# Gate sigmoids and scaled keys computed where their tiles leave PSUM, with the conv norm, the scan's steps and the final scaling dealt out differently

## The chip, the cores and the metric

The kernel runs on one core of a Trainium2 chip. The metric is device time in microseconds (us) for one execution. In what follows PE is TensorE (matrix products into PSUM banks), DVE is VectorE, ACT is ScalarE, POOL is GpSimd, and SP is the engine whose queue issues most of the transfers between SBUF and DRAM.

## The reference

The program is one layer of an encoder on x of 1024 positions and 1024 channels, float32. A projection h W_in feeds a convolution module and a two-direction gated scan; their merge goes back through W_out, and a gated feed-forward part follows.

```python
h = rmsnorm(x); proj = h @ w_in               # columns: glu, q, v, z_f, z_b, og, g_a, g_b
a = glu(glu_in)                               # 512 channels
a = depthwise_conv31(a); a = silu(layernorm(a)); a = a @ pw_w
for z, lb in ((z_f, lb[0]), (z_b, lb[1])):    # 8 heads of 128 channels, each direction
    f   = lb + (1 - lb) * sigmoid(z)          # forget gate, clipped to [1e-6, 1]
    key = (1 - lb) * sigmoid(-z)
    o  += scan(silu(q) * 128**-0.5, key, v, log(clip(f)))
o = rmsnorm(o) * norm_w * silu(og) @ o_w
x = x + (sigmoid(g_a) * a + sigmoid(g_b) * o) @ w_out
x = x + ffn(rmsnorm(x)); out = rmsnorm(x)
```

## The kernel before

All activations lie transposed: channels on the 128 partitions, positions along the free axis in two halves of 512. A number of full precision is kept as two parts (a rounded high part, and the rest), and a product of two such numbers takes three matmuls (`mm3`, L149 to L151). `split` (L125) makes the parts: a CAST on ACT for the high part, a TENSOR_TENSOR on DVE for the low part.

The projection's 128-column tiles are listed in `todo`, in the order in which they are computed: q and og of the eight heads, then v, z_f and z_b head by head, then the merge gates. The first 38 tiles are computed two at a time as 19 "pairs" (`in_pair`, `pair_job`). A pair multiplies a 2 by 2 block of tiles with seven block products instead of eight, each product 12 matmuls of 128x512. The products run in the order 1, 2, 6, 7, 5, 4, 3 and use three PSUM banks: mm, tr, mm, sc, mm, sc, mm. Products that add on to a bank wait until ACT has copied its value before (`A.copy` into `su`, L440). DVE or ACT then finishes the four result tiles (`evac`), and SP stores them to DRAM. Every tile of z is stored raw into `d_z`.

The order on the engines is that in which the program emits its instructions, apart from some that a scheduler may move (`pin` fixes one in its place). Two kinds of work are woven by hand: a `Stream` such as `s_pairs` holds the pieces of the dense products, and `fill(n)` emits n pieces of it between pieces of other work. A piece of a pair is two groups of three matmuls. `later(n, f)` (the list `chores`) calls f after n further pieces. Beside the pairs run the depthwise convolution on DVE (31 taps on 1024 positions, four chunks of channels), and then, for each half, the conv's layer norm. The norm loads four chunks (`cx`) from `d_cv` with SP (L1061), sums them on DVE (L1051, L1053), multiplies by a matrix of ones on PE for the mean (L1065), subtracts, squares on ACT (L1071), forms the reciprocal deviation, multiplies and shifts on DVE, applies silu on ACT (L1079), splits into two parts (`ch`) and stores these to `d_ca` (L1082). The `cx` pages are two buffers of two chunks, so that the loads of the second half follow the last read of the first.

The scan (`scan_inputs`, `Base`, `scan_levels`, `scan_states`, 16 rounds of head and half) follows, woven with the dense tiles that are left (`dense.fill`). `scan_inputs` loads q and the two z tiles; ACT makes sigmoid(-z) (L1163), sigmoid(z) (L1164) and the affine gate (L1165), DVE the clamp and the scaling of the key. `Base` prepares levels of doubling block sizes 1 to 16; `scan_levels` goes on with 32 and 64, with small matmuls on PE (`blocks`, L1281), each after a DVE step `double` that scales keys and queries. At the program's end the down projection's last tiles are transposed back (`turn_out`, L1890), squared and summed on ACT (L1892), and scaled by the final norm's factor (`scale_out`: 640 columns on DVE, L1928, and 384 on ACT, L1926), once all eight column tiles of a part are there.

Of the kernel before, what the change touches and what calls it, by code (L numbers as in the profile page):

```python
# [24 lines left out]
LN_LAST = 12  # L25
# [5 lines left out]
BASE_STEPS = 1  # L31
# [17 lines left out]
def tile_hybrid_encoder(  # L49
# [107 lines left out]
    chores = []  # L157
# [5 lines left out]
    def advance_chores(n=1):  # L163
        for c in list(chores):
            c[0] -= n
            if c[0] <= 0:
                chores.remove(c)
                c[1]()

# [395 lines left out]
    d_z = scratch("d_z", 2, NH, 2)  # L565
# [230 lines left out]
    def store(dst, func=None):  # L796
# [12 lines left out]

    todo = [  # L810
# [7 lines left out]
    todo += [  # L818
        t
        for h in range(NH)  # L820
        for t in (
            (OFF_V + h * DK, store(d_v[h])),
            (OFF_ZF + h * DK, store(d_z[0][h])),
            (OFF_ZB + h * DK, store(d_z[1][h])),
        )
    ]
    todo += [(OFF_GA + i * P, store(d_ga[i], AF.Sigmoid)) for i in range(ND)]
# [162 lines left out]

    def lb_of(d, h):
        return lbw[:, 2, d * NH + h : d * NH + h + 1]
# [63 lines left out]
    for half in range(2):  # L1056
# [18 lines left out]
        rs = next(rstd)  # L1075
        for j, xn in enumerate(xs):
            V.tensor_tensor(xn, xn, rs, op=ALU.mult)
            V.tensor_scalar(xn, xn, vec("lnw", j), vec("lnb", j), op0=ALU.mult, op1=ALU.add)
            A.activation(xn, xn, AF.Silu)  # L1079
            both = gp0.tile([P, 2, H], F32R, tag="gl", name=nm("ch"), bufs=NCW)  # L1080
            for dst, part in zip(d_ca[j][half], split(both[:, 0, :], both[:, 1, :], xn, V)):
                nc.sync.dma_start(dst, part.bitcast(F32))  # L1082
        s_pairs.fill(LN_LAST)
# [62 lines left out]
    kscale = cp.tile([P, 2 * NH], F32, name="kscale")  # L1146
    V.tensor_scalar(kscale, lbw[:, 3, :], DK**-0.5, None, op0=ALU.mult)

# [3 lines left out]
    def scan_inputs(i):  # L1152
# [7 lines left out]
        for d in range(2):  # L1160
            z = page(hp, "zi", 3)
            nc.sync.dma_start(z, d_z[d][h][half])
            A.activation(kG[:, d, :], z, AF.Sigmoid, scale=-1.0)  # L1163
            A.activation(z, z, AF.Sigmoid)  # L1164
            A.activation(f[:, d, :], z, AF.Identity, scale=oml_of(d, h), bias=lb_of(d, h))  # L1165
        V.tensor_scalar(f, f, MIN_FORGET, 1.0, op0=ALU.max, op1=ALU.min)
        return q, f, kG, kscale[:, h : h + NH + 1 : NH]
# [49 lines left out]
    def scan_base(ins):  # L1217


        q, f, kG, ks = ins  # L1220
        qF = hp.tile([P, 2, H], F32, tag="qF", name=nm("qF"), bufs=4)
        D_t = hp.tile([P, 4, 32], F32, tag="D", name=nm("D"), bufs=3)
        for d in range(2):
            V.tensor_scalar(kG[:, d, :], kG[:, d, :], ks[:, d : d + 1], None, op0=ALU.mult)
# [45 lines left out]
    def scan_levels(base, S_t, Tt):  # L1270
# [25 lines left out]
        level(slot(b, 1), A16, row(Q16))  # L1296
# [743 lines left out]
```

## Time and profile before

| | us |
|---|---|
| median of 3 runs (lowest, highest) | 1740.16 (1738.36, 1743.63) |
| the profiled execution, its own time | 1736.41 |
| its span, first to last instruction | 1734.3 |
| PE busy | 1709.2 |
| DVE busy | 1255.9 |
| ACT busy | 830.3 |
| POOL busy | 170.4 |

The granted PE clock was 0.998 of full speed. Rows of the profile name the line, the engine, the operation and the tiles (out<-in, buffer numbers left out). A row of a timeline begins with its start and its length in us, and has in brackets how long the engine had been idle and who ended that. A matmul of 128x512 is listed with some 0.39 us because matmuls are pipelined; how often one starts is what counts. The pairs take the stretch from some 118 to 490 us, the scan that from 490 to 880.

### The profile page before, as it was taken

The numbers are of one execution on the slowest core, as the hardware profiler recorded it, in microseconds if no ns is written. First come the engines' busy times: TensorE is split into PE (matmuls) and PEld (weight loads), VectorE is DVE, ScalarE is ACT, GpSimd is POOL, SyncE is SP. The second block draws the span as 40 slices with busy tenths as digits, with TensorE's granted clock in tenths as the row PEclk, the third lists the DMA queues.
The fourth block names the chain that finished last, engine by engine and source line by source line (L and its number), as shares of the span: only waits on it lengthen the run. The fifth ranks groups of instructions, "written<-read, shape, count | busy, mean of one in ns | idle before, by whom it ended". The sixth has DMA issues, their size and how long they took to land.

```text
span 1734.3 us, 30669 instructions
## 1 busy us (share of the span) xinstructions
PE 1709.2 (99%) x11902; PEld 1415.0 (82%) x11902; DVE 1255.9 (72%) x1937; ACT 830.3 (48%) x1544; POOL 170.4 (10%) x185
## 2 busy tenths in 40 slices
PE   8999999999999999999999999999999999999997
PEld 6878888888788888888878888888888888888787
DVE  5599999746778888888557466667767776657865
ACT  7444443334566777776442245444434433542334
POOL 2211111100000000000000002011111111000110
PEclk9999999999999999999999999999999999999999
DMA  8768888854673444435579466568777776783842
GB/s 288 239 167 184 193 194 193 197 167 154 207 230 104 131 126 132 127 115 192 175 248 333 147 207 205 146 148 170 158 170 160 180 172 153 229 267 107 205 91 98
DMA packets 343751, 308.27 MB, mean 178 GB/s; under 512 B 25262, under 2 KB 255798, under 8 KB 343606
## 3 DMA queue, kind: packets, MB, share of 16 engines
q1 hardware_dynamic: 289590, 267.51, 48.7%
q0 software_dynamic: 44800, 37.76, 15.2%
q10 hardware_dynamic: 9216, 1.05, 0.4%
q8 instruction: 93, 1.52, 0.4%
q14 instruction: 52, 0.43, 0.1%
HBM read 201.40 MB, written 87.03 MB: 166 GB/s over the span
## 4 chain that ended last, share of the span: by engine, by line
PE 44%; DMA 2%; DVE 2%; ACT 1%; issue 1%; SPq 0%; POOL 0%; POOLq 0%; ACTq 0%; DVEq 0%
PE mm L151 10%; PE mm L150 10%; PE mm L149 10%; PE sc L149 3%; PE sc L150 3%; PE sc L151 3%; PE tr L149 1%; PE tr L150 1%; PE tr L151 1%; DMA tm<-d_bm 1%; DVE hx L125 0%; DMA wr<-in_ffn_w_down_dram 0%; DMA wr<-wr 0%; DMA d_gc<-ft 0%; DVE wp L125 0%
## 5 line engine op out<-in xcount | busy, mean ns | idle before, releaser
L149 PE MATMUL mm<-hx,wp 128*128 128x512 f32 x1068 | 428.0, 401 | 3.3 <-ACT tm L851 2.1
L151 PE MATMUL mm<-hx,wp 128*128 128x512 f32 x1068 | 418.1, 391 | 0.9 <-DVE wp L125 0.8
L150 PE MATMUL mm<-hx,wp 128*128 128x512 f32 x1068 | 416.9, 390 | 0.3 <-DVE hx L125 0.2
L125 ACT CAST wp<-wr 128x1024 fp32r<-128x1024 f32 (+2 forms) x147 | 147.2, 1002 | 259.2 <-PE mm L150 119.5
L151 PEld LDWEIGHTS mm<-hx,wp 128*128 128x128 f32 x1068 | 200.9, 188 | 46.3 <-DVE wp L125 3.4
L149 PEld LDWEIGHTS mm<-hx,wp 128*128 128x128 f32 x1068 | 200.8, 188 | 46.1 <-ACT tm L851 2.6
L150 PEld LDWEIGHTS mm<-hx,wp 128*128 128x128 f32 x1068 | 201.2, 188 | 41.3 <-DVE hx L125 1.6
L125 DVE TENSOR_TENSOR wp<-wr,wp 128x1024 fp32r<-128x1024 f32 (+2 forms) x145 | 169.3, 1168 | 68.5 <-ACT wp L125 67.9
L1039 DVE SCALAR_TENSOR_TENSOR acc<-gl,v_b,acc 128x1024 f32<-128x1024 f32 x120 | 148.9, 1277 | 0.4
L1144 DVE TENSOR_TENSOR qF<-qF,tb 128x512 f32<-128x512 f32 x96 | 65.0, 684 | 20.8 <-ACT A L1176 20.7
L440 ACT COPY su<-mm 128x512 f32<-128x512 f32 x82 | 47.7, 582 | 66.2 <-PE mm L151 66.2
L149 PE MATMUL tr<-hx,wp 128*128 128x512 f32 x180 | 70.5, 392 | 0.0
L125 ACT CAST wq<-sw 128x1024 fp32r<-128x1024 f32 x41 | 43.2, 1053 | 56.3 <-PE mm L150 40.5
L151 PE MATMUL tr<-hx,wp 128*128 128x512 f32 x180 | 70.1, 389 | 0.0
L150 PE MATMUL tr<-hx,wp 128*128 128x512 f32 x180 | 70.0, 389 | 0.0
L1636 DVE SCALAR_TENSOR_TENSOR tm<-gp,v_a,tm 128x512 f32<-128x512 f32 x88 | 65.9, 749 | 3.9 <-ACT tm L1634 2.0
L1144 DVE TENSOR_TENSOR kG<-kG,tb 128x512 f32<-128x512 f32 x96 | 65.1, 684 | 3.7 <-PE sc L1281 3.7
L149 PE MATMUL mm<-hy,wp 128*128 128x512 f32 x164 | 64.2, 391 | 0.0
L149 PE MATMUL sc<-hy,wq 128*128 128x512 f32 x164 | 64.2, 391 | 0.0
L151 PE MATMUL sc<-hy,wq 128*128 128x512 f32 x164 | 63.8, 389 | 0.0
L150 PE MATMUL mm<-hy,wp 128*128 128x512 f32 x164 | 63.8, 389 | 0.0
L150 PE MATMUL sc<-hy,wq 128*128 128x512 f32 x164 | 63.8, 389 | 0.0
(372 smaller groups left out, 3609.9 us busy)
## 6 DMA issues: line engine op xcount, KB each, us to landing
wr<-in_w_in_dram SPq DMA_DIRECT2D x48, 512.0 KB
wr<-in_ffn_w_up_dram SPq DMA_DIRECT2D x22, 512.0 KB
sw<-in_w_in_dram SPq DMA_DIRECT2D x38, 256.0 KB
d_g<-ft SPq DMA_DIRECT2D x38, 256.0 KB
sw<-in_ffn_w_up_dram SPq DMA_DIRECT2D x38, 256.0 KB
sw<-in_ffn_w_up_dram POOLq DMA_DIRECT2D x19, 512.0 KB, 8.1
wr<-sw POOLq DMA_DIRECT2D x32, 256.0 KB, 3.8
wr<-wr POOLq DMA_DIRECT2D x32, 256.0 KB, 4.1
```

What stands on the lines that cost most here:

```text
L125: parts = A.copy(hi, src), eng.tensor_tensor(lo, src, hi.bitcast(F32), op=ALU.subtract)
L149: T.matmul(acc, whi[:, k, :], ahi, start=first, stop=False, skip_group_check=again)
L150: T.matmul(acc, whi[:, k, :], alo, start=False, stop=False, skip_group_check=again)
L151: T.matmul(acc, wlo[:, k, :], ahi, start=False, stop=last, skip_group_check=again)
L440: A.copy(t, acc)
L1039: V.scalar_tensor_tensor(acc, g[:, k : k + S], tap(k), acc, op0=ALU.mult, op1=ALU.add)
L1144: V.tensor_tensor(o, a, b, op=op)
L1636: V.scalar_tensor_tensor(c, g[:, o + k : o + k + H], vec("fdw", k * NF + j), c, op0=ALU.mult, op1=ALU.add,)
```

## The change

The two sigmoids, the affine gate, the clamp and the key's scaling move from the scan's inputs to the pairs. `store_gates` is the new evacuation of a z tile. It puts three ACT steps into `paced`, a queue from which `advance_chores` takes one step per piece; the clamp follows two pieces after the last. Results go to two scratch tensors, `d_f` and `d_k`, each as large as `d_z` was, and the scan loads these two. Keys take pages of the tag "gl" (four buffers, also used by the norm's `ch`) for heads 1 to 6, and temporary pages for heads 0 and 7. For head 0 the scaling is on ACT and the clamp on POOL, for the others both are on DVE. `todo` now has six v tiles after q and og, then 14 z tiles (heads 0 to 6, pairs 11 to 17, pairs counted from 0), then two v tiles (pair 18); head 7's z tiles come among the dense tiles.

In the conv norm the 12 pieces that followed the second half of the norm in one go are dealt out: one after each chunk's multiply and shift, two after all four silus, one and a half after each chunk's parts. In the scan the blocks of 32 come in the step of the levels 8 and 16, their predicated copies and `double(32)` behind them, and two empty steps follow before the blocks of 64; the preparation of the next round but one begins a step earlier. At the end a turned tile of two chunks comes six pieces after its sums instead of four, and the final scaling takes one chunk per six pieces instead of two or four.

Here is ACT in the conv norm's first half in pairs 15 and 16, before: from the silus (L1079, on `cx`) to the two copies `su` of pair 16's third and fourth product.

```order
L1079 ACTIVATE cx_3622<-cx_3622 128x512 x2
L125 CAST ch_3823<-cx_3622 128x512
L125 CAST ch_3831<-cx_3622 128x512
L125 CAST wp_3892<-wr_3884 128x1024
L1079 ACTIVATE cx_3625<-cx_3625 128x512
L125 CAST ch_3839<-cx_3625 128x512
L1079 ACTIVATE cx_3625<-cx_3625 128x512
L125 CAST ch_3847<-cx_3625 128x512
L440 COPY su_3926<-mm_3855 128x512
L440 COPY su_3940<-sc_3857 128x512
```

And the same place in the changed kernel, where the silus are on L1129 and the gates' steps on L824 (sigmoid(-z) into `kp`), L827 (sigmoid(z) into `ev`) and L834 (affine gate); `su_4079` is the copy of pair 16's third product.

```order
L827 ACTIVATE ev_3949<-ev_3949 128x512
L824 ACTIVATE kp_4011<-mm_3778 128x512
L834 ACTIVATE ev_3949<-ev_3949,lbw 128x512
L1129 ACT_TABLE_LOAD
L1129 ACTIVATE cx_3745<-cx_3745 128x512
L827 ACT_TABLE_LOAD
L827 ACTIVATE ev_3977<-mm_3778 128x512
L1129 ACT_TABLE_LOAD
L1129 ACTIVATE cx_3745<-cx_3745 128x512
L1129 ACTIVATE cx_3748<-cx_3748 128x512 x2
L124 CAST wp_4036<-wr_4028 128x1024
L441 COPY su_4079<-mm_3978 128x512
```

The silus moved together, three loads of a function table came among them and the gates' steps, and the norm's casts into `ch` moved behind the copy.

The second place is SP's queue between the first half's parts and the second half's loads, before:

```order
L1082 DMA d_ca_0_1_121<-ch_3823 128x512
L1082 DMA d_ca_0_1_125<-ch_3831 128x512
L1082 DMA d_ca_0_0_128<-ch_3839 128x512
L1082 DMA d_ca_0_1_129<-ch_3839 128x512
L1082 DMA d_ca_0_0_132<-ch_3847 128x512
L1082 DMA d_ca_0_1_133<-ch_3847 128x512
L806 DMA d_z_5_0_242<-ev_3911 128x512
L1061 DMA cx_3969<-d_cv_1_113 128x512
L1061 DMA cx_3969<-d_cv_1_115 128x512
L1061 DMA cx_3972<-d_cv_1_117 128x512
L806 DMA d_z_5_1_259<-ev_3954 128x512
L1061 DMA cx_3972<-d_cv_1_119 128x512
```

and after:

```order
L1122 DMA d_ca_0_1_125<-ch_4090 128x512
L841 DMA d_f_4_1_241<-ev_3977 128x512
L835 DMA d_k_5_0_274<-kp_4072 128x512
L1122 DMA d_ca_0_0_128<-ch_4112 128x512
L1122 DMA d_ca_0_1_129<-ch_4112 128x512
L1122 DMA d_ca_0_0_132<-ch_4124 128x512
L1122 DMA d_ca_0_1_133<-ch_4124 128x512
L841 DMA d_f_5_0_242<-ev_4055 128x512
L1103 DMA cx_4148<-d_cv_1_113 128x512
L1103 DMA cx_4148<-d_cv_1_115 128x512
L1103 DMA cx_4151<-d_cv_1_117 128x512
L1103 DMA cx_4151<-d_cv_1_119 128x512
```

The gates' stores `d_f` and `d_k` came among the stores of the parts, and the loads of `cx` stand behind all of them; in the kernel before the queue had one z store ahead of them.

The diff:

```diff
@@ -22,13 +22,12 @@
 CONV_FILL = 1.67
 NPAIRS = 19
 LN_FILL = 6
-LN_LAST = 12
+LN_STEP = 1.5
 GLU_FIRST = 4
 GLU_LEAD = 6
 GLU_FILL = 2
 GLU_MORE = 4
 GLU_LATE = 17
-BASE_STEPS = 1
 ALIGN = 128
 H = 512
 EPS = 1e-6
@@ -154,7 +153,7 @@
 
 
 
-    chores = []
+    chores, paced = [], collections.deque()
 
     def later(n, do):
 
@@ -166,6 +165,8 @@
             if c[0] <= 0:
                 chores.remove(c)
                 c[1]()
+        if paced:
+            paced.popleft()()
 
     class Weights:
 
@@ -562,7 +563,8 @@
     d_q = scratch("d_q", NH, 2)
     d_v = scratch("d_v", NH, 2)
     d_og = scratch("d_og", NH, 2)
-    d_z = scratch("d_z", 2, NH, 2)
+    d_f = scratch("d_f", 2, NH, 2)
+    d_k = scratch("d_k", 2, NH, 2)
     d_bm = scratch("d_bm", NH, 2)
     d_x0 = dp.tile([P, 4, ND, P], F32, name="d_x0")
     d_xt = [[d_x0[:, :, k, :], scratch(f"d_xt_{k}")] for k in range(ND)]
@@ -807,6 +809,41 @@
 
         return evac
 
+    def gl_page():
+        return gp0.tile([P, 2, H], F32, tag="gl", name=nm("kp"), bufs=NCW)[:, 0, :]
+
+    def store_gates(d, h, key_page):
+        def evac(half, x0, x1=None, op=None):
+            f, x, key = ev(), x0, []
+            if x1 is not None:
+                V.tensor_tensor(f, x0, x1, op=op)
+                x = f
+
+            def complement():
+                key.append(key_page())
+                pin(A.activation(key[0], x, AF.Sigmoid, scale=-1.0))
+
+            def forget():
+                pin(A.activation(f, x, AF.Sigmoid))
+                if h == 0:
+                    pin(A.activation(key[0], key[0], AF.Copy, scale=kscale_of(d, h)))
+                else:
+                    pin(V.tensor_scalar(key[0], key[0], kscale_of(d, h), None, op0=ALU.mult))
+
+            def bound():
+                pin(A.activation(f, f, AF.Identity, scale=oml_of(d, h), bias=lb_of(d, h)))
+                nc.sync.dma_start(d_k[d][h][half], key[0])
+                later(2, clamp)
+
+            def clamp():
+                eng = G if h == 0 else V
+                pin(eng.tensor_scalar(f, f, MIN_FORGET, 1.0, op0=ALU.max, op1=ALU.min))
+                later(1, lambda: nc.sync.dma_start(d_f[d][h][half], f))
+
+            paced.extend((complement, forget, bound))
+
+        return evac
+
     todo = [
         t
         for h in range(NH)
@@ -815,15 +852,14 @@
             (OFF_OG + h * DK, store(d_og[h], AF.Silu)),
         )
     ]
-    todo += [
-        t
+    values = [(OFF_V + h * DK, store(d_v[h])) for h in range(NH)]
+    gate_tiles = [
+        (off + h * DK, store_gates(d, h, gl_page if 0 < h < NPAIRS - 12 else tmp))
         for h in range(NH)
-        for t in (
-            (OFF_V + h * DK, store(d_v[h])),
-            (OFF_ZF + h * DK, store(d_z[0][h])),
-            (OFF_ZB + h * DK, store(d_z[1][h])),
-        )
+        for d, off in enumerate((OFF_ZF, OFF_ZB))
     ]
+    n = 2 * (NPAIRS - 12)
+    todo += values[:-2] + gate_tiles[:n] + values[-2:] + gate_tiles[n:]
     todo += [(OFF_GA + i * P, store(d_ga[i], AF.Sigmoid)) for i in range(ND)]
     todo += [(OFF_GB + i * P, store(d_gb[i], AF.Sigmoid)) for i in range(ND)]
 
@@ -988,6 +1024,12 @@
     V.tensor_tensor(lbw[:, 2, :], lbw[:, 1, :], lbw[:, 1, :], op=ALU.subtract)
     V.tensor_scalar(lbw[:, 3, :], lbw[:, 2, :], -1.0, 1.0, op0=ALU.mult, op1=ALU.add)
 
+    kscale = cp.tile([P, 2 * NH], F32, name="kscale")
+    V.tensor_scalar(kscale, lbw[:, 3, :], DK**-0.5, None, op0=ALU.mult)
+
+    def kscale_of(d, h):
+        return kscale[:, d * NH + h : d * NH + h + 1]
+
     def lb_of(d, h):
         return lbw[:, 2, d * NH + h : d * NH + h + 1]
 
@@ -1073,14 +1115,22 @@
         next(rstd)
         s_pairs.fill(5)
         rs = next(rstd)
+
+        def store_parts(j):
+            both = gp0.tile([P, 2, H], F32R, tag="gl", name=nm("ch"), bufs=NCW)
+            for dst, part in zip(d_ca[j][half], split(both[:, 0, :], both[:, 1, :], xs[j], V)):
+                nc.sync.dma_start(dst, part.bitcast(F32))
+
         for j, xn in enumerate(xs):
             V.tensor_tensor(xn, xn, rs, op=ALU.mult)
             V.tensor_scalar(xn, xn, vec("lnw", j), vec("lnb", j), op0=ALU.mult, op1=ALU.add)
+            s_pairs.fill()
+        for xn in xs:
             A.activation(xn, xn, AF.Silu)
-            both = gp0.tile([P, 2, H], F32R, tag="gl", name=nm("ch"), bufs=NCW)
-            for dst, part in zip(d_ca[j][half], split(both[:, 0, :], both[:, 1, :], xn, V)):
-                nc.sync.dma_start(dst, part.bitcast(F32))
-        s_pairs.fill(LN_LAST)
+        s_pairs.fill(2)
+        for j in range(NCW):
+            store_parts(j)
+            s_pairs.fill(LN_STEP)
     s_pairs.drain()
     p1.release()
     gp0.release()
@@ -1143,9 +1193,6 @@
     def tt(o, a, b, op=ALU.mult):
         V.tensor_tensor(o, a, b, op=op)
 
-    kscale = cp.tile([P, 2 * NH], F32, name="kscale")
-    V.tensor_scalar(kscale, lbw[:, 3, :], DK**-0.5, None, op0=ALU.mult)
-
     def c4(t):
         return t.rearrange("p (c t) -> p c t", c=4)
 
@@ -1158,13 +1205,9 @@
         kG = hp.tile([P, 2, H], F32, tag="kG", name=nm("kG"), bufs=3)
         nc.sync.dma_start(q, d_q[h][half])
         for d in range(2):
-            z = page(hp, "zi", 3)
-            nc.sync.dma_start(z, d_z[d][h][half])
-            A.activation(kG[:, d, :], z, AF.Sigmoid, scale=-1.0)
-            A.activation(z, z, AF.Sigmoid)
-            A.activation(f[:, d, :], z, AF.Identity, scale=oml_of(d, h), bias=lb_of(d, h))
-        V.tensor_scalar(f, f, MIN_FORGET, 1.0, op0=ALU.max, op1=ALU.min)
-        return q, f, kG, kscale[:, h : h + NH + 1 : NH]
+            nc.sync.dma_start(f[:, d, :], d_f[d][h][half])
+            nc.sync.dma_start(kG[:, d, :], d_k[d][h][half])
+        return q, f, kG
 
     def pairs(t, h, other=H):
 
@@ -1217,11 +1260,9 @@
     def scan_base(ins):
 
 
-        q, f, kG, ks = ins
+        q, f, kG = ins
         qF = hp.tile([P, 2, H], F32, tag="qF", name=nm("qF"), bufs=4)
         D_t = hp.tile([P, 4, 32], F32, tag="D", name=nm("D"), bufs=3)
-        for d in range(2):
-            V.tensor_scalar(kG[:, d, :], kG[:, d, :], ks[:, d : d + 1], None, op0=ALU.mult)
         k_d, Q1 = page(hp, "A", 8), page(hp, "A", 8)
         tt(k_d, kG[:, 0, :], kG[:, 1, :], ALU.add)
         A1 = woven(kG, 1)
@@ -1294,15 +1335,16 @@
         b = bank("ob")
         level(slot(b, 0), A8, row(Q8))
         level(slot(b, 1), A16, row(Q16))
+        S_b = bank("sc")
+        for at, g, _ in each():
+            T.matmul(S_b[g, at : at + 32], none, none, start=True, stop=True)
+        blocks(S_b, 32)
         for n, m in enumerate((m_8, m_16)):
             V.copy_predicated(D_t, over(m), near(slot(b, n)))
-        yield
-        b = bank("sc")
-        for at, g, _ in each():
-            T.matmul(b[g, at : at + 32], none, none, start=True, stop=True)
-        blocks(b, 32)
         tb = double(tb, 32)
         yield
+        yield
+        b = S_b
         blocks(b, 64)
         double(tb, 64, view(Tt, 0, [[4, 2], [1, 4]]))
         A.copy(S_t, c4(b))
@@ -1438,11 +1480,12 @@
 
     NI = 2 * NH
     cur = Base(scan_inputs(0))
-    ins = scan_inputs(1)
+    ahead = Base(scan_inputs(1))
     dense.fill(7)
     for pieces in (3, 4, 4, 3, 0):
         cur.step(1)
         dense.fill(pieces)
+    ahead.step(1)
     pending = Stream(iter(()))
     for h in range(NH):
         Tt = hp.tile([P, 2, 2, 4], F32, tag="Tt", name=nm("Tt"), bufs=4)
@@ -1452,14 +1495,14 @@
         for half in range(2):
             i = 2 * h + half
             base = cur.result()
-            ahead = Base(ins) if i + 1 < NI else None
-            ins = scan_inputs(i + 2) if i + 2 < NI else None
-
-            def between(fill):
-                dense.fill(fill)
-                if ahead is not None:
-                    ahead.step(BASE_STEPS)
+            following = Base(scan_inputs(i + 2)) if i + 2 < NI else None
+
+            def between(n):
+                dense.fill(FILL)
                 pending.fill(1)
+                step_of = ahead if n < 4 else following
+                if step_of is not None:
+                    step_of.step(1)
 
             S_t = hp.tile([P, 4, P], F32, tag="S", name=nm("S"), bufs=3)
             vl = load(d_v[h][half])
@@ -1470,12 +1513,12 @@
                         T.transpose(b[:, c * P : (c + 1) * P], vl[:, c * P : (c + 1) * P], ident)
                     v = hp.tile([P, 4, DK], F32, tag="v", name=nm("v"), bufs=3)
                     A.copy(v.rearrange("p c e -> p (c e)"), b)
-                between(FILL)
+                between(n)
             qF, kG = base[:2]
-            for _ in scan_states(i, kG, v, Tt, Sf, Sb):
-                between(FILL)
+            for n, _ in enumerate(scan_states(i, kG, v, Tt, Sf, Sb)):
+                between(3 + n)
             kept.append((S_t, v, qF))
-            cur = ahead
+            cur, ahead = ahead, following
         pending = Stream(outputs(h, kept, Tt, Sf, Sb))
 
     dense.owed = 0
@@ -1877,7 +1920,7 @@
     def final_evac(i, half, chunks, acc):
         t = xr[i][half][:, chunks[0] * P : (chunks[-1] + 1) * P]
         V.tensor_tensor(t, acc, t, op=ALU.add)
-        later(4, lambda: turn_out(i, half, chunks))
+        later(8 - len(chunks), lambda: turn_out(i, half, chunks))
 
     def turn_out(i, half, chunks):
 
@@ -1998,8 +2041,8 @@
     fy = tc.alloc_tile_pool(name="fy", bufs=1, reuse_waits="tile")
     st = Stream(run_jobs(last_jobs(LAST0, final_evac)))
     for n, part in enumerate(PARTS[:-1]):
-        st.fill(4 * ND * (n + 1) + 3 - st.count)
-        finish(*part, late=2 + 2 * n)
+        st.fill(4 * ND * (n + 1) + (3, 5)[n] - st.count)
+        finish(*part, late=6)
     st.drain()
     advance_chores(1 << 10)
     finish(*PARTS[-1], late=0)
```

## The prediction

> **What bounds the kernel now.** I read the page's first part, then busy time by stretch, then what TensorE (PE) waited for, then single instructions around each place that the change touches.
>
> ```profile
> span 1734.3 us, 30669 instructions
> PE 1709.2 (99%) x11902; PEld 1415.0 (82%) x11902; DVE 1255.9 (72%) x1937; ACT 830.3 (48%) x1544; POOL 170.4 (10%) x185
> ```
> ```profile
> 118.00:309.00 191.00, 190.24 (x840) 157.24 (x839) 189.17 (x198) 77.41 (x107) 33.26 (x30) 1.00 0.82 188
> 309.00:490.00 181.00, 180.16 (x794) 147.33 (x793) 109.95 (x138) 71.67 (x109) 11.92 (x13) 1.00 0.64 190
> 490.00:880.00 390.00, 387.59 (x5951) 325.88 (x5950) 305.60 (x665) 271.62 (x611) 14.70 (x16) 1.00 0.46 144
> ```
>
> The columns of the three stretches are length, then PE, PEld, DVE, ACT and POOL busy, the clock granted, DMA share and GB/s. The first two are the column pairs, the third the scan with its dense tiles. PE never stops: 840 matmuls in 190.24 us are 0.2265 us each, so a product of 12 takes 2.72 us and a pair of seven products 19.03 us. The change leaves every matmul of the 11902 in place. A time can therefore only come from PE's waits, removed or added. These are the waits that PE has near the edited code:
>
> ```profile
> PE sc L1281 <- DVE qF L1144: 2.0, 2, 1.0
> PE sc L1890 <- ACT y L1926: 1.5, 1, 1.5
> PE mm L149 <- DVE ev L800: 0.8, 1, 0.8
> PE mm L149 <- ACT su L440: 0.7, 1, 0.7
> PE sc L1329 <- ACT kT L1322: 0.3, 1, 0.3
> ```
>
> Columns: total, times, longest, in us. Everything that could be gained stands here; it is about 5.3 us. So the question is what the new work on ACT, DVE and SP makes PE wait for.
>
> **The time of one ACT step.** Next come ACT, DVE and SP rows with min/median/max in ns, or start and length in us.
>
> ```profile
> L1163 ACT ACTIVATE kG<-zi x32: 613/636/657, 490.8 to 801.7; 128x512 f32<-128x512 f32 x32
> L1165 ACT ACTIVATE f<-zi,lbw x32: 800/812/857, 493.1 to 803.4; 128x512 f32<-128x512 f32 x32
> L440 ACT COPY su<-mm x7: 567/589/590, 405.5 to 469.1; 128x512 f32<-128x512 f32 x7
> L125 ACT CAST wp<-wr 128x1024 fp32r<-128x1024 f32 x4 | 4.2, 1046 | 3.7 <-PE mm L150 3.7
> L1079 ACT ACTIVATE cx<-cx 128x512 f32<-128x512 f32 x4 | 2.4, 627 | 2.2 <-DVE cx L1078 2.2
> L125 ACT CAST wq<-w 128x512 fp32r<-128x512 f32 x2 | 1.2, 624 | 2.2 <-PE sc L151 2.2
> 119.03 1.28 ACT L985 ACT_TABLE_LOAD   x1
> 120.33 0.21 ACT L985 ACTIVATE lbw<-su 128x16 f32<-128x16 f32 x1
> 434.95 0.39 PE L151 MATMUL sc<-hy,wq 128*128 128x512 f32 x1
> 436.08 0.50 PE L149 MATMUL mm<-hy,wq 128*128 128x512 f32 x1 [0.74 <-ACT su L440]
> 1084.13 0.86 PE ob L601 x2
> L125 POOL TENSOR_TENSOR hx<-ev,hx 128x512 fp32r<-128x512 f32 x8 | 11.1, 1386 | 22.0 <-ACT hx L125 22.0
> ```
>
> A sigmoid costs 0.63, the Identity with scale and bias 0.81, a silu 0.63, a weight cast 1.05 (0.62 for half the width), a copy `su` 0.59, a table load 1.28. Each pair's products write, in order, the banks mm, tr, mm, sc, mm, sc, mm. The third product adds on to what the first left in mm and so waits for the copy of the first; the fifth waits for the copy of the third. Before, that last wait once cost 0.74 us (436.08; from start to start 1.13, which is 0.9 above a matmul's 0.23), because the silus and casts of the conv norm stood ahead of the copy.
>
> **Pair 12.** The built order of the changed kernel has on ACT, from the half cast that waits for the end of pair 11's sixth product: cast 0.62, table load 1.28, two sigmoids 1.26, cast 1.05, sigmoid 0.63, scaling 0.6, Identity 0.81, sigmoid 0.63, scaling 0.6, Identity 0.81, sigmoid 0.63, copy 0.59: 9.5 us. PE wants the copy after three products, 8.2. Wait 1.3, with 0.02 us of issue per step 1.5. This is head 0, whose scalings are on ACT. Its four clamps on POOL have no row; the nearest, a POOL operation of that size, takes 1.39. They lie beside an idle POOL: nothing taken, 1.4 at the upper end, where a weight load queues on SP behind the store that waits for the clamp, and nothing to gain.
>
> **Pair 16 (conv norm, first half).** ACT from the same point, the end of pair 15's sixth product: cast 0.62, Identity 0.81, two sigmoids 1.26, sigmoid 0.63, cast 1.05, Identity 0.81, sigmoid 0.63, copy `tm` 0.59, Identity 0.81, sigmoid 0.63, copy 0.59 for the third product: 8.4, in time for 9.0 (three products and the 0.86 of the norm's broadcast matmul, 1084.13 being the same code). But then, ahead of the copy for the fifth product: two sigmoids 1.26, Identity 0.81, load 1.28, silu 0.63, load 1.28, sigmoid 0.63, load 1.28, three silus 1.88, cast 1.05, copy 0.59: 10.7. It ends at 19.1, and PE wants it at 5 products and 0.86, that is 14.5. Wait 4.6; the 0.9 that stands there now goes into it, so net +3.7. Bounds: 3.2 if the rows ahead are not late, 5.2 with issue steps.
>
> By the Trainium skill's ScalarE: Activation LUTs, What ACT_TABLE_LOAD costs, a switch is 1283 ns of load plus about 1380 ns of drain. The load agrees; the drain doesn't show, since L985's own instruction starts 0.02 us behind its load. With the drain the six added loads would weigh double, which is a rival below.
>
> **Pair 17 (the mean of the second half).** This is the largest term. The loads of the next half's conv chunks (cx) stand on SP behind the stores of the norm's parts.
>
> ```profile
> 431.72 5.34 SPq L1082 DMA_DIRECT2D d_ca<-ch  x8
> 438.32 1.39 SPq L1061 DMA_DIRECT2D cx<-d_cv  x3
> 440.31 0.43 SPq L1061 DMA_DIRECT2D cx<-d_cv  x1
> 442.59 0.69 DVE L1051 TENSOR_TENSOR tm<-cx 128x512 f32<-128x512 f32 x1 [1.33 <-DMA cx<-d_cv]
> 449.86 1.02 PE L1065 MATMUL ob<-tm,ones_m 128*128 128x512 f32 x2
> ```
> ```profile
> 433.69 1.22 DVE L125 TENSOR_TENSOR wp<-wr,wp 128x1024 fp32r<-128x1024 f32 x1
> 434.83 0.69 DVE L125 TENSOR_TENSOR ch<-cx,ch 128x512 fp32r<-128x512 f32 x1
> 435.43 0.68 DVE L298 TENSOR_TENSOR wr<-wr,sw 128x512 f32<-128x512 f32 x1
> 437.95 0.32 SPq L806 DMA_DIRECT2D d_z<-ev  x1
> 889.87 3.15 DMA d_a<-ev
> 893.58 4.97 DMA tm<-d_bm
> ```
>
> Now the loads go out at 438.3, eleven us ahead of the mean matmul (449.86), which waits for nothing. In the changed order, counted from the end of pair 16's sixth product: ACT does half cast, Identity, table load, sigmoid, weight cast, 4.4; `ch` of chunk 0 to 5.0. DVE's lower weight part (1.22) to 5.6, lower `ch` part (0.69) to 6.3; SP issues its store (0.32) at 6.6. Four `ch` pages are now shared with the gates' keys, and chunk 3 reuses chunk 0's: it waits for that store to land, 3.15 as d_a's of equal size, 9.8. ACT's cast to 10.4. DVE has meanwhile the next weight part and one sum (1.22 + 0.68) from 9.3 to 11.2; then chunk 3's lower part to 11.9. Only then may SP issue that store, a gate store and four loads: 2.5 us, to 14.4. In the rows above the first two loads (two thirds of 1.39, so to 439.25) served a sum at 442.59: 3.3 us. So 17.7, a last sum 18.4. PE is ready at three products, 8.2. **Wait 10.2**; with issue steps 10.5 taken. Ends: 9 if the loads land 1.2 us sooner (an earlier store gains nothing, as DVE holds chunk 3's lower part to 11.2), 13 if store and loads take the 4.97 of the slowest transfer of this size.
>
> By the Trainium skill's DMA: Bandwidth & Descriptors, Anatomy of one DMA (written for transfers that GpSimd issues), a transfer costs about 2.0 us plus its bytes at 436 GB/s, an estimate of 2.6 us for 256 KB. The trace has 3.15 and 3.3; by the page's figure the loads land 0.7 sooner and this wait would be 9.5.
>
> **Pair 18 (second half).** Same point, same rows up to the third product's copy: 8.4. Then two sigmoids 1.26, Identity 0.81, sigmoid 0.63, load 1.28, silu 0.63, Identity 0.81, three silus 1.88, copy 0.59: 16.3 against 14.5. +1.8 (1.5 to 2.2). In pairs 13 to 15 the same count leaves about 1 us to spare; 0.2 taken in all.
>
> **The scan.** Identity, two sigmoids and clamps leave ACT and DVE, 271.62 and 305.60 busy of 390: not PE's path, worth nothing alone. What PE waits for is the second matmul set on `sc`:
>
> ```profile
> 630.01 0.69 PE L1281 MATMUL sc<-qF,kG 128*64 128x64 f32 x16 [1.03 <-DVE qF L1144]
> 1701.48 2.13 ACT L1926 ACTIVATE y<-y,frs 128x384 f32<-128x384 f32 x4 [0.47 <-POOL frs L1902]
> 1703.27 0.41 PE L1890 MATMUL sc<-ident,xr 128*128 128x128 f32 x2 [1.54 <-ACT y L1926]
> ```
>
> Two dense portions now stand between it and the doubling that it needs, instead of one. Its 2.0 goes. PE's idle time in the whole stretch is 390.00 − 387.59 = 2.4; at 436.08 the loss was 0.16 above the wait, and with six places in the stretch where PE's starts lie 0.2 or more too far apart (the two of L1281 the largest) that is 1.0 to 1.2 besides: 3.6 taken, 2.0 to 4. Loads of a scan input go from 32 to 64 and their stores likewise; at a DMA share of 0.46 and with two halves' lead nobody waits. **The end.** The four final scalings, 2.13 in one block, are dealt out a chunk per six pieces: the 1.54 goes, nothing follows the last matmul that wasn't there. Pair 9's 0.8 stays; it stands ahead of all moved work.
>
> **Sum:** 1.5 + 3.7 + 10.5 + 1.8 + 0.2 − 3.6 − 1.5 = **+12.6**. Against the profiled execution's own 1736.41 (span and 2.1 around it) that gives 1749.0; that execution is 3.7 under the runs' median 1740.16, which would give 1752.8. I take 1751. 0.3% is 5.2 us, about what a measurement can tell from no change.
>
> **Rivals.**
> - *The mean doesn't wait* (0.13). If chunk 3's page is free by about 5 us, because the store lands early and DVE has a hole, loads leave some six us sooner and the term of 10.5 shrinks to 0 to 5: 1739 to 1745. For it: before, they were eleven us early. Against: three queues in a row.
> - *ACT is never late* (0.12), the other side. ACT is busy 71.67 of 181 us; it decides if its chains are 4.6 us shorter than counted, that is without the three loads around the silus, or begin that much sooner. Then pairs 12, 16 and 18 cost nothing, the parts leave in time for the mean too, and only the gains remain, pair 16's present 0.9 among them: −3.6 − 1.5 − 0.9 = −6.0, 1730 to 1734.
> - *Loads cost double* (0.10): 1.3 more for one load in pair 12, three in 16, one each in 17 and 18 is +7.8: 1759. This is the skill's drain, as a mechanism of this kernel; L985's row speaks against it.
> - *The scan's waits only move* (inside the forecast): the 3.6 doesn't come, 1755.
>
> **Chances.** Forecast, 1745 to 1757: 0.65, all slower; loads double 0.10, slower; mean doesn't wait 0.13, within 0.3%; never late 0.12, faster. The range from 1740 to 1760 leaves out the faster case, some of the mildest second and a slice above.
>
> **What would show it.** Right: PE's waits list has the mean's matmul behind DVE's sum at some 10 us, once; `su` copies at 1.5, 4.6 and 1.8; L1281's and L1890's entries gone; twelve table loads. Wrong: the mean's matmul without a wait, or the load of cx landing while PE still works on pair 17's first product. Most exposed is the landing time of a 256 KB store, which stands twice in one chain.

## The result

The changed kernel takes 1750.88 us (median of 6 runs, 1747.86 to 1752.75), the kernel before 1738.91 (6 runs, 1735.01 to 1743.63). The ratio is 1.0067, with a 95% interval from 1.0048 to 1.0086: slower, by 12 us. The profiled execution took 1747.86, its span is 1746.1.

### The profile page after: what moved, and what is told of

Read it like the earlier page. It is cut to its first block, busy times and chain, and to the rows that moved or that the text cites. A ratio compares the mean times of both kernels' runs of the same rounds, so it can differ in the third digit from the quotient of the medians.

```text
span 1746.1 us, 30858 instructions
## 1 busy us (share of the span) xinstructions
PE 1705.2 (98%) x11902; PEld 1416.4 (81%) x11902; DVE 1257.3 (72%) x1945; ACT 831.4 (48%) x1543; POOL 178.1 (10%) x189
## 3 DMA queue, kind: packets, MB, share of 16 engines
q8 instruction: 93, 1.52, 0.4%
## 5 line engine op out<-in xcount | busy, mean ns | idle before, releaser
L1194 DVE TENSOR_TENSOR qF<-qF,tb 128x512 f32<-128x512 f32 x96 | 65.7, 686 | 18.4 <-ACT A L1219 17.7
L148 PE MATMUL mm<-hy,wp 128*128 128x512 f32 x164 | 65.3, 398 | 1.2 <-ACT su L441 1.2
L441 ACT COPY su<-mm 128x512 f32<-128x512 f32 x82 | 47.3, 577 | 38.8 <-PE mm L150 38.5
L148 PE MATMUL sc<-hy,wq 128*128 128x512 f32 x164 | 64.2, 391 | 0.0
L150 PE MATMUL mm<-hy,wp 128*128 128x512 f32 x164 | 64.1, 391 | 0.0
L149 PE MATMUL mm<-hy,wp 128*128 128x512 f32 x164 | 64.1, 391 | 0.0
L150 PE MATMUL sc<-hy,wq 128*128 128x512 f32 x164 | 63.8, 389 | 0.0
```

Of the source, the lines that this page charges most:

```text
L148: T.matmul(acc, whi[:, k, :], ahi, start=first, stop=False, skip_group_check=again)
L149: T.matmul(acc, whi[:, k, :], alo, start=False, stop=False, skip_group_check=again)
L150: T.matmul(acc, wlo[:, k, :], ahi, start=False, stop=last, skip_group_check=again)
L441: A.copy(t, acc)
L1194: V.tensor_tensor(o, a, b, op=op)
```

## The profile after

What PE waited for in the changed kernel; the entries L1281 and the scaling `y` of the list before are gone, and two large ones are new:

```profile
PE ob L1107 <- DVE tm L1095: 12.8, 1, 12.8
PE mm L148 <- ACT su L441: 6.4, 5, 4.2
PE sc L1933 <- ACT oj L1935: 0.7, 1, 0.7
```

L1107 is the mean's matmul of the conv norm's second half. L441 is the copy `su`; its longest wait, 4.2, is pair 16's fifth product.

All 11902 matmuls are in both traces, and their order is the same up to the scan, so the start of the same matmul can be compared. The three boundaries are the first matmul of pair 0's second product, the 2101st matmul (pairs done) and the 8471st (scan done); the last stretch ends with the last matmul's start.

| stretch, us | before | after | difference |
|---|---|---|---|
| start to pair 0 | 118.19 | 116.10 | −2.1 |
| pairs | 365.67 | 390.91 | +25.2 |
| scan and its dense tiles | 487.24 | 478.41 | −8.8 |
| from there to the last matmul | 754.64 | 752.89 | −1.8 |

The first stretch is the same code in both. In the other runs of this study it lies between 115.8 and 118.6, so the −2.1 belongs to no part of the change. The −1.8 of the last stretch is no larger than chance either: two executions of one kernel (the norm as before, below) have 754.8 and 751.7 there. Behind the last matmul's start the program ends after 8.6 us before and 7.8 after.

How the mean came to wait, in the timeline of SP, ACT, DVE and PE:

```profile
458.89 3.00 SPq L1122 DMA_DIRECT2D d_ca<-ch  x4
460.20 0.62 ACT L124 CAST ch<-cx 128x512 fp32r<-128x512 f32 x1 [1.82 <-DMA d_ca<-ch]
460.85 0.69 DVE L124 TENSOR_TENSOR ch<-cx,ch 128x512 fp32r<-128x512 f32 x1 [0.49 <-ACT ch L124]
462.45 2.09 SPq L1103 DMA_DIRECT2D cx<-d_cv  x4
467.24 0.69 DVE L1093 TENSOR_TENSOR tm<-cx 128x512 f32<-128x512 f32 x1 [0.45 <-DMA cx<-d_cv]
468.86 1.42 DVE L1095 TENSOR_TENSOR tm<-tm,cx 128x512 f32<-128x512 f32 x2 [0.93 <-DMA cx<-d_cv]
470.33 1.22 PE L1107 MATMUL ob<-tm,ones_m 128*128 128x512 f32 x1 [12.80 <-DVE tm L1095]
```

Chunk 3's cast waits for the landing of chunk 0's store, since they share a page; its lower part follows, then the last stores, then the four loads, then the sums. PE had nothing to do from 457.5 on.

The windows of the same stretch show two things more. The columns are PE, PEld, DVE, ACT and POOL busy, granted clock, DMA share, GB/s; the last row is of the kernel before, where its loads of `cx` are under way:

```profile
434.00:457.00 23.00, 18.78 (x72) 14.95 (x71) 11.85 (x18) 15.87 (x22) 0.00 (x0) 0.85 0.32 104
457.00:470.00 13.00, 0.53 (x3) 0.10 (x1) 8.54 (x15) 6.67 (x10) 0.00 (x0) 0.63 1.01 371
470.00:475.00 5.00, 4.67 (x11) 3.06 (x12) 3.53 (x7) 1.83 (x3) 0.00 (x0) 0.61 0.30 116
475.00:480.00 5.00, 5.00 (x24) 4.11 (x23) 1.91 (x3) 1.81 (x3) 0.00 (x0) 1.00 0.00 0
```
```profile
438.00:443.00 5.00, 5.00 (x23) 4.12 (x23) 2.32 (x3) 1.68 (x2) 0.00 (x0) 1.00 0.91 299
```

The 16 DMA engines are full while PE waits (share 1.01), but they were nearly full in the kernel before too (0.91), without a wait. And the clock granted to PE is 0.61 on average in the five us after the wait: 11 matmuls in 5 us, where 24 start in the next 5.

## The experiments

### The scan's regrouping alone

The kernel before, with the diff's parts on `scan_levels` and on the scan's loop, and nothing else:

```diff
         level(slot(b, 1), A16, row(Q16))
+        S_b = bank("sc")
...
+        blocks(S_b, 32)
...
-            ahead = Base(ins) if i + 1 < NI else None
-            ins = scan_inputs(i + 2) if i + 2 < NI else None
+            following = Base(scan_inputs(i + 2)) if i + 2 < NI else None
```

> The kernel before with the scan's regrouping alone (blocks of 32 in the step of levels 8 and 16, two empty steps before the blocks of 64, the next preparation begun a step earlier); gates, conv norm and end as before. Forecast's theory: only PE's shown waits go, 3.6 us, so about 1735 where the kernel before has 1739. Theory from the trace after, where the scan is 8.8 us shorter but its pauses of 0.2 and more only 2.9: the rest comes from fewer changes between dense and small matmuls, so the gain is 8 to 9 us, about 1730. Rival: the regrouping needs ACT and DVE freed of the gates, then no gain or a loss, 1738 to 1743, with DVE or ACT as releaser of waits on the small matmuls.

Measured: 1737.97 against 1738.39, ratio 0.9995 (0.9983 to 1.0008). The forecast's theory falls, and so does that of a gain of 8 to 9 us from fewer changes alone: the stretch of the scan took 488.9, 1.7 more than before. (In the traces whose scan is the old one, before and with the norm or the end alone, it lies between 487.2 and 489.1.) The waits at the blocks of 64 did go, but PE waits elsewhere in the scan:

```profile
PE tr L1321 <- DVE kG L1144: 5.4, 4, 2.2
PE sc L1195 <- ACT A L1176: 1.9, 2, 1.6
PE sc L1330 <- ACT kT L1323: 1.1, 2, 0.7
```

DVE's doubling of the keys and ACT's copies come too late for what is now asked earlier: the rival. PE's listed waits in this stretch are 9.7 us in all, against 3.0 before.

### The gates moved, the scan's order as before

The changed kernel without the two parts of the run above:

```diff
-        blocks(S_b, 32)
...
+        blocks(b, 32)
...
+                if ahead is not None:
+                    ahead.step(BASE_STEPS)
...
-                step_of = ahead if n < 4 else following
```

> The changed kernel with the scan's order as before (blocks of 32 and 64 a step apart, next preparation begun at the round's start); gates, conv norm and end as changed. Theory that the scan's 8.8 us need both parts, the freed ACT and DVE and the regrouping: here the waits on DVE at the blocks of 64 go for the most part (2 to 3 us), the rest stays lost, so the scan is 5 to 7 us longer than in the changed kernel: 1755 to 1758. Rival that the freed engines give it all: 1750 to 1752. Rival that they give nothing: 1759 or more.

Measured: 1762.17 against 1739.89, ratio 1.0129 (1.01 to 1.0158), 22 us above the kernel before, where the changed kernel is 12 above it: the rival that the freed engines give nothing. The scan took 488.2, as long as with the gates in it, and the old wait is still there (L1281 before, L1323 here):

```profile
PE sc L1323 <- DVE qF L1195: 2.9, 3, 1.0
```

So the freed engines alone give nothing (0.9 longer than before), the regrouping alone gives nothing (1.7 longer), and both together give 8.8. In the eight further runs with both the scan took 7.4 to 10.5 less than before.

### The dealing out of the conv norm alone

```diff
+            s_pairs.fill()
+        for xn in xs:
             A.activation(xn, xn, AF.Silu)
...
-        s_pairs.fill(LN_LAST)
+        s_pairs.fill(2)
+        for j in range(NCW):
+            store_parts(j)
+            s_pairs.fill(LN_STEP)
```

> The kernel before with the conv norm's pieces dealt out alone; z stored raw, scan and end as before. Theory that the mean's wait of 12.8 us needs the gates (shared key pages, gate stores ahead on SP, loads of the function table): no wait at the mean over 1 us, time within 2 us of before. Rival that dealing out alone makes the loads of cx late: a wait of 5 us or more at the mean, time 1744 or more.

Measured: 1739.1 against 1738.39, ratio 1.0008 (0.9991 to 1.0025). PE's waits from 400 to 490 us are this one line:

```profile
PE mm L149 <- ACT su L440: 0.4, 1, 0.4
```

Without the gates the dealing out costs nothing that shows, and the mean has no wait.

### The parts stored in one go

The changed kernel, with the pieces behind the parts instead of between them:

```diff
-        s_pairs.fill(2)
         for j in range(NCW):
             store_parts(j)
-            s_pairs.fill(LN_STEP)
+        s_pairs.fill(8)
```

> The changed kernel with the four parts of the conv norm stored in one go right after the silus, the pieces that stood between them behind them (eight in one go). Theory that the mean waits because the loads of cx stand behind the last part's store: the loads leave some 7 us earlier, the wait of 12.8 falls to 3 or less and PE's slow stretch behind it goes (1.8), while four casts more ahead of the copy add about 2.5 to the wait of pair 16: 1738 to 1741. Rival that the DMA engines are the limit there (their share is 1.01 while PE waits): the loads land late all the same, the wait stays above 6, time 1746 or more.

Measured: 1739.36 against 1738.39, ratio 1.0012 (0.9997 to 1.0027). The loads of `cx` left at 445.93, PE reached the mean's matmul at 460.79 without a wait, and the longest wait of the copy rose from 4.2 to 6.3:

```profile
PE mm L148 <- ACT su L441: 10.6, 5, 6.3
```

The pairs fell from 390.9 to 380.6. As the theory had it: where the loads stand in SP's queue decides on the mean's wait. The DMA engines were full here too while the loads were under way (share 1.03), so that alone doesn't make the wait:

```profile
445.00:450.00 5.00, 5.00 (x13) 3.87 (x13) 1.70 (x3) 0.33 (x2) 0.00 (x0) 0.52 1.03 343
```

### The silus held together

```diff
         for xn in xs:
-            A.activation(xn, xn, AF.Silu)
+            pin(A.activation(xn, xn, AF.Silu))
```

> The changed kernel with the conv norm's four silus held together, so that two of the three table loads ahead of pair 16's copy go. Theory by the sum of ACT's steps: its wait falls from 4.2 to about 1.6 (two loads of 1.28), the mean's wait stays between 11 and 13.5, time 1747 to 1749. Rival that a switch of tables costs a drain of about its own length as well: the wait goes altogether, time 1745 or less. Rival that the wait isn't ACT's steps but what they wait for: it stays above 3.

Measured: 1750.35 against 1738.39, ratio 1.0065 (1.0048 to 1.0083); the median isn't told from the changed kernel's, though the profile shows what was expected:

```profile
PE ob L1107 <- DVE tm L1095: 12.8, 1, 12.8
PE mm L148 <- ACT su L441: 7.0, 5, 2.6
```

Pair 16's copy is waited for 2.6 instead of 4.2. That is 1.6 for two loads of 1.28; ACT lost most of the rest of their 2.56 to a new pause of 1.15, where a sigmoid waited for its page's store to land. (The time expected, 1747 to 1749, was missed.)

```profile
435.42 0.60 ACT L827 ACTIVATE ev<-mm 128x512 f32<-128x512 f32 x1 [1.15 <-DMA d_f<-ev]
```

In the changed kernel a load costs its own length: in the rows below each ACTIVATE starts 0.02 behind its load, and the load between them 0.01 behind the instruction ahead of it.

```profile
432.70 1.28 ACT L1129 ACT_TABLE_LOAD   x1
434.00 0.63 ACT L1129 ACTIVATE cx<-cx 128x512 f32<-128x512 f32 x1
434.64 1.28 ACT L827 ACT_TABLE_LOAD   x1
435.94 0.60 ACT L827 ACTIVATE ev<-mm 128x512 f32<-128x512 f32 x1
```

The Trainium skill's ScalarE: Activation LUTs, What ACT_TABLE_LOAD costs, gives 1283 ns and about 1380 ns of drain; of these only the first shows here.

### The conv norm as before, the rest as changed

The changed kernel with the norm's loop of the kernel before (silu, parts and stores chunk by chunk, then twelve pieces):

```diff
-            s_pairs.fill()
-        for xn in xs:
             A.activation(xn, xn, AF.Silu)
...
-        s_pairs.fill(2)
-        for j in range(NCW):
-            store_parts(j)
-            s_pairs.fill(LN_STEP)
...
+        s_pairs.fill(LN_LAST)
```

> The changed kernel with the conv norm written as in the kernel before (silu, parts and stores chunk by chunk, then twelve pieces in one go); gates in the pairs, scan and end as changed. Theory that the dealing out makes the mean wait once the gates are there: loads of cx leave in pair 16, no wait at the mean over 1 us, and pair 16's copy comes after one table load instead of three, a wait of 1 to 2; with the scan 8.8 shorter that gives 1732 to 1735. Rival that the gates alone load ACT and SP too much in these pairs: the mean waits 5 or more, 1742 or more.

> The lump run's kernel once more with more rounds, to tell it from the kernel before: 1734 to 1737, a ratio of 0.998 whose interval stays under 1, if the 3.8 us seen there are its own; 1738 or more if they were chance.

Measured: 1736.14 against 1739.89, ratio 0.9982 (0.9966 to 0.9997); again, in 12 runs, 1734.66 against 1737.95, ratio 0.9984 (0.997 to 0.9997). This version is faster than the kernel before by 3 to 4 us, and so than the changed kernel by some 15. The mean has no wait, the scan keeps its 8.9, and the pairs take 10.8 more than before, not 25.2. What is left of waits from 430 to 500 us in the first execution:

```profile
PE sc L148 <- ACT su L441: 3.0, 1, 3.0
PE mm L148 <- ACT su L441: 2.4, 3, 1.0
PE mm L148 <- DVE ev L802: 0.9, 1, 0.9
```

In the first set that is less gain than expected (1732 to 1735): the 3.0 at the copy from sc, behind one table load and four gate steps, was not in the sum.

### Less work for ACT in that version

The silu as x times sigmoid(x), so that no table is loaded for it, with the product on DVE:

```diff
-            A.activation(xn, xn, AF.Silu)
+            gate_of = tmp()
+            A.activation(gate_of, xn, AF.Sigmoid)
+            V.tensor_tensor(xn, xn, gate_of, op=ALU.mult)
```

> As the run before it, and the conv norm's silu made as x times sigmoid(x), the product on DVE, so that no table is loaded for it (six table loads instead of ten in the program). Theory by the sum of ACT's steps: no wait at pair 16's copy (13.2 us of steps against 14.5), nor at pair 18's; 2 to 3 us less than the run before it, 1729 to 1732, below the kernel before. Rival that DVE, with four products more per half, holds the sums or parts: waits on DVE of 2 or more in pairs 15 to 18, 1733 or more.

Measured: 1740.49 against 1739.89, ratio 1.0008 (0.9996 to 1.002). The copies' waits nearly went (0.7 from 430 to 500), and DVE's evacuations took their place:

```profile
PE mm L148 <- DVE ev L819: 4.5, 1, 4.5
PE mm L148 <- DVE ev L802: 4.4, 1, 4.4
```

Then the product on POOL, the affine gate on DVE instead, and both:

```diff
-            V.tensor_tensor(xn, xn, gate_of, op=ALU.mult)
+            G.tensor_tensor(xn, xn, gate_of, op=ALU.mult)
...
-                pin(A.activation(f, f, AF.Identity, scale=oml_of(d, h), bias=lb_of(d, h)))
+                if h == 0:
+                    pin(A.activation(f, f, AF.Identity, scale=oml_of(d, h), bias=lb_of(d, h)))
+                else:
+                    pin(V.tensor_scalar(f, f, oml_of(d, h), lb_of(d, h), op0=ALU.mult, op1=ALU.add))
```

> The run with the norm as before and x times sigmoid(x), but with that product on POOL, idle there, instead of DVE. Theory that DVE's four products more per half held the evacuations in that run (4.5 us twice): these waits fall under 2, and as no table is loaded the copies' waits are those of the lump run less 1.3 each: 1731 to 1735. Rival that the chain of sigmoid, product and parts is too long wherever the product is made, since DVE's parts stand in its queue ahead of the evacuation: the waits on DVE stay above 3, 1738 or more.

> The run with the norm as before, and the affine gate (0.81 on ACT, one per tile of z) on DVE for heads 1 to 6. Theory that ACT's sum of steps sets the copies' waits: each of pairs 13 to 18 has 1.6 to 3.2 less ahead of its copies, the 3.0 on the copy from sc falls below 2, 1732 to 1735. Rival that DVE, which then does gate and clamp, is late with evacuations: waits on DVE of 2 or more, 1737 or more.

> Both of these together: product of x and sigmoid on POOL, affine gate on DVE. If ACT's steps are what PE waits for, it has the least of the waits on copies, under 2 in all from pair 12 on, and 1729 to 1733; if DVE's queue is, as much as the worse of the two alone, 1737 or more.

Measured: 1742.86 against 1738.5, ratio 1.003 (1.0014 to 1.0046); 1736.95, ratio 0.999 (0.9977 to 1.0002); 1739.18, ratio 1.0003 (0.9988 to 1.0017). These are, in this order, the product on POOL, the gate on DVE, and both. None is shown to be better than the version with the norm as before. With the product on POOL the evacuation was waited for 6.2, with the gate on DVE the sums of squares (L613) 4.5, with both the evacuation 4.3:

```profile
PE mm L148 <- DVE ev L819: 6.2, 1, 6.2
```
```profile
PE ob L613 <- DVE tm L1098: 4.5, 2, 2.8
```

So the rivals hold, with the gate on DVE by its waits (1736.95 is a hair under the rival's 1737). The window of pair 16 from 436 to 442 us, in the version with the norm as before and in that with the product on DVE (busy PE, PEld, DVE, ACT), fits that: ACT is busy 5.66 of 6 us in the one, DVE 6.00 of 6 in the other.

```profile
436.00:442.00 6.00, 5.25 (x23) 4.03 (x22) 4.76 (x8) 5.66 (x9) 0.00 (x0) 1.00 0.92 332
```
```profile
436.00:442.00 6.00, 6.00 (x28) 4.99 (x27) 6.00 (x11) 3.84 (x9) 0.00 (x0) 1.00 0.86 290
```

### The end alone

```diff
-        later(4, lambda: turn_out(i, half, chunks))
+        later(8 - len(chunks), lambda: turn_out(i, half, chunks))
...
-        finish(*part, late=2 + 2 * n)
+        finish(*part, late=6)
```

> The kernel before with the end's change alone (turned tiles six pieces after their sums, a chunk's final scaling per six pieces). Forecast's theory: the 1.5 of PE waiting for the scaling goes and nothing takes its place, 1.5 less, which the interval may just show. Theory from the trace after: 0.7 of wait on the squares and 0.3 more in the last transpose remain, 0.5 to 1.0 less, not told from no change. Rival that the tail behind the last matmul grows as the scalings are put off: 1 or more slower.

Measured: 1736.19 against 1737.95, ratio 0.9992 (0.9975 to 1.0008): not told from no change. The wait of 1.5 at the transposes is replaced by one of 0.7 on the squares:

```profile
PE sc L1890 <- ACT oj L1892: 0.7, 1, 0.7
```

## Why the prediction was right, and where its terms were not

- **The total.** +12.6 was forecast on the profiled execution, 1751 in all; measured are +11.5 on the profiled executions (1747.86 against 1736.41) and 1750.88. That it came so close is partly luck. The pairs took 25.2 more, where 17.7 was forecast, and the scan gave 8.8, where 3.6 was: two errors of opposite sign. The 2.1 of the first stretch belongs to neither.
- **The premise.** "A time can therefore only come from PE's waits" and "everything that could be gained stands here; it is about 5.3 us" did not hold. The scan alone gave 8.8. The change keeps the number of matmuls but not their order in the scan, and the order has a price of its own (see the scan below); and behind a long wait PE starts its matmuls more slowly.
- **Pair 17, the mean.** Right as a mechanism, link by link: page, cast, lower part, stores, loads, sums. 12.8 instead of 10.5. Counted from the end of pair 16's sixth product (449.2), the steps came at 12.3 for chunk 3's lower part (forecast 11.9) and 15.3 for the last load's issue (14.4), so the first links held within 0.9. What was too small is the landing. The 3.3 was read at the first two of the four loads before, and put on the last one. By the landing events of that trace the third and fourth load took 3.7 and 4.1 us from the end of their issue, with four and five other transfers of SP's queue still under way. After, the last load took 4.9 (464.5 to 469.4), with six under way. With the parts stored in one go, where three or four were under way, the four loads took 3.0 to 3.5. The upper end of 13 allowed for it.
- **Pairs 12, 16 and 18.** 1.5, 4.6 and 1.8 forecast; 0.6, 4.2 and 0.5 measured, each in its place and with twelve table loads in all, as counted. The sums of ACT's steps were too long: where one step follows another it starts some 0.1 us before the end of the one ahead (489.61 with 0.81, and the next at 490.33), while the forecast added 0.02 per step. Pair 12's chain took 8.7 instead of 9.5, pair 18's 14.1 instead of 16.3. That pair 16 came out at 4.2 all the same is luck: its steps were shorter too, but ACT stood idle for 2.20 among them until DVE's evacuation came (429.85), and this pause was in no sum.

```profile
429.85 0.63 ACT L824 ACTIVATE kp<-ev 128x512 f32<-128x512 f32 x1 [2.20 <-DVE ev L819]
```
```profile
489.61 0.81 ACT L834 ACTIVATE ev<-ev,lbw 128x512 f32<-128x512 f32 x1
490.33 0.62 ACT L827 ACTIVATE ev<-ev 128x512 f32<-128x512 f32 x1
```

- **What was missing from the pairs.** The slow clock after the two long waits: behind the 4.2 a dozen matmuls start 0.43 apart instead of 0.23, behind the 12.8 the mean's two passes and the next four are slow, together some 4.5 us. And small waits on copies: 0.4 at pair 13's fifth product, where 0.2 was taken for three pairs, and 0.6 at pair 16's third. Each of the short waits costs 0.27 more than its length from start to start.
- **The scan.** The step that failed is "Identity, two sigmoids and clamps leave ACT and DVE: not PE's path, worth nothing alone". True alone, as the run with the old order shows; but the regrouping needs them gone, and then the scan gives 8.8 where 3.6 was forecast. The starts of its matmuls take this apart. From one matmul to the next the distance depends on the kinds of the two: from a dense one it is 0.227 us to another dense one, 0.23 to one of 128 columns, 0.32 to one of 32 or 64; from one of 32 it is 0.13 to one of 128. There were 50 places of a dense one followed by one of 32 or 64 columns before, and 19 after. If every kind of neighbours is counted at its usual distance, the new order takes some 5.0 us less: an estimate from the starts in ten of the traces, 4.7 to 5.1 by what is taken as usual. The run with the regrouping alone has this order as well: its listed waits are 6.7 above those before, yet its scan is only 1.7 longer, which leaves the same 5.0. The run with the old order has the 50 places of before, and its scan is as long as before. The other 3.9 are pauses beyond the usual distances. The listed waits fell only from 3.0 to 2.1, and the rest is spread over many small ones; what ended these is not shown.
- **The end.** −1.5 forecast; its wait fell from 1.5 to 0.7, and the whole stretch by 1.8, of which the run with the end alone shows nothing certain.
- **The rivals.** The mean waits, so "the mean doesn't wait" falls. PE waits for a copy by ACT at five places, so "ACT is never late" does. Loads don't cost double, and in the changed kernel the scan's gain came; that its waits only move is what happened with the regrouping alone.

## What to carry to other kernels

When work moves off a part of the program, count what it does to the order where it lands: here 12 pieces of cover were dealt out between a chain of stores, and the loads behind them in the queue arrived 13 us late. The landing time of such a load should be read at a load with as many transfers still under way. Freed engines were worth nothing here until the order was changed to use them, and the changed order nothing until they were freed; test the two together and apart. Keeping every matmul does not keep PE's time: their order counts. A wait of PE costs more than its length when the clock drops behind it (2.7 us more behind the 4.2).

## What was not expected of the hardware

- **PE's clock drops after a wait.** Behind each of the ten waits of 4.2 to 12.8 us, in seven kernels, the next matmuls started 0.43 us apart, for 3 to 6 us; the rows of the changed kernel after its wait of 4.2, and the window after that of 12.8 (0.61, above), are examples:

```profile
440.98 0.80 PE L148 MATMUL mm<-hy,wq 128*128 128x512 f32 x1 [4.22 <-ACT su L441]
441.58 0.63 PE L149 MATMUL mm<-hy,wq 128*128 128x512 f32 x1
442.00 0.63 PE L150 MATMUL mm<-hy,wq 128*128 128x512 f32 x1
442.43 0.63 PE L148 MATMUL mm<-hy,wq 128*128 128x512 f32 x1
```

  For shorter waits it is open what decides. Behind six of 1.7 to 2.9 us the granted clock fell to a half for 3.4 us or more (1.7 and 2.8 with the gate on DVE, 2.1 with the parts in one go, 2.2 with the product on POOL, 2.2 with the regrouping alone, 2.9 with the norm as before); behind others (2.0, twice 2.2, 2.3, 2.6, 3.0) it stayed full. The 2.9 and the 3.0 are the same matmul of the same kernel in two executions:

```profile
444.41 0.79 PE L148 MATMUL sc<-hx,wq 128*128 128x512 f32 x1 [2.86 <-ACT su L441]
445.01 0.63 PE L149 MATMUL sc<-hx,wq 128*128 128x512 f32 x1
```
```profile
445.87 0.50 PE L148 MATMUL sc<-hx,wq 128*128 128x512 f32 x1 [2.97 <-ACT su L441]
446.21 0.39 PE L149 MATMUL sc<-hx,wq 128*128 128x512 f32 x1
```

  The Trainium skill's TensorE: Matmul & The Clock Gate, What's actually happening, puts the limit at one idle window of about 3.4 us that runs freely. The waits from 4.2 on agree with it; the six shorter ones do not, so a wait below 3.4 us is not safe here.
- **DVE slows while POOL works.** With the product of the silu on POOL, the shift of a chunk on DVE, 0.54 before, took up to 1.52, and the lower part, 0.69 before, up to 1.77; the weight part between POOL's two stretches took its usual 1.21 (at 437.44):

```profile
L1120 DVE TENSOR_SCALAR cx<-cx,v_a x4: 537/1026/1519, 432.4 to 436.0; 128x512 f32<-128x512 f32 x4
L1123 POOL TENSOR_TENSOR cx<-cx,tm x4: 1279/1601/2072, 433.7 to 439.7; 128x512 f32<-128x512 f32 x4
L124 DVE TENSOR_TENSOR ch<-cx,ch x4: 679/1215/1774, 438.6 to 443.8; 128x512 fp32r<-128x512 f32 x4
```

  So idle time of POOL is no free place for a product next to a full DVE.
